# Gated DeltaNet in a two-layer encoder: the scale of the key products from a reciprocal of the sum of squares

## The chip, the cores and the metric

The kernel runs on one core of a Trainium2 chip. The metric is the device time of one execution in microseconds (us), the median of several runs. The engines are named as the profile names them: PE (TensorE matmuls), PEld (its weight loads), DVE (VectorE), ACT (ScalarE), POOL (GpSimd) and SP (SyncE, which issues the transfers).

## The reference

Two layers of an encoder work on 256 frames of width 1024 in float32. Each layer is a SwiGLU half-step, a mixing step (differential attention, a Mamba-2 head group and a gated DeltaNet head group side by side, between one input and one output projection), and a second SwiGLU half-step, with a layer norm behind each. Only the DeltaNet part is touched:

```python
def l2_normalize(x):
    return x * lax.rsqrt(jnp.sum(x * x, -1, keepdims=True) + 1e-6)

q = l2_normalize(q.reshape(bsz, s_len, G_HEADS, G_DK)) * (G_DK ** -0.5)
k = l2_normalize(k.reshape(bsz, s_len, G_HEADS, G_DK))
...
kb = kc * bc[..., None]                 # bc is beta, per frame and head
lmat = jnp.where(strict, jnp.einsum('bhcld,bhcsd->bhcls', kb, kc) * decay, 0.0)
imat = jnp.eye(CHUNK, dtype=jnp.float32) + lmat
u = lax.linalg.triangular_solve(imat, vb, left_side=True, lower=True, unit_diagonal=True)
...
v_new = u_i - jnp.einsum('bhld,bhdv->bhlv', w_i, st)
```

There are 4 heads of width 64 and chunks of 64 frames. The normalisation of k enters the products k k^T twice, so what scales them is beta / (sum of squares + 1e-6).

## The kernel before

Everything is float32. A large projection splits each weight tile into a high and a low part (`wh` by ACT in L250, `wl` by DVE in L251) and multiplies both by the high part of the activations, and `wh` also by their low part. PE is fed by such products almost all the time: L327 and L342 to L345 for the input projections, L238 to L245 for the output projections. The mixing work of a layer (attention, Mamba, DeltaNet) is written as Python generators ("chains") that are stepped between the weight units of the input projection. A `yield` with a number puts the rest of a chain that much later on a modelled clock; `until(key)` holds it until another chain has left a tile under that key. What comes out is one instruction list per engine, and each engine runs its list in order, waiting on semaphores.

The chain in question is `delta`. In both layers it does this:

- `ssps` (PE, by the helper `mm` whose line is L389): sums of squares of k and q per frame and head, as products with a selector of two columns. `ss` (DVE, L658) is that plus 1e-6, 128x16: 8 columns for k and 8 for q.
- `r8` (POOL, L660) is `ss` to the power -1/2 for all 16 columns.
- `products(b)` makes `laps`, the products k k^T and k q^T of the block `b` of 128 frames, in two PSUM tiles from the four-buffer pool `aux`, one for each half of the 128 partitions. In the program `products(1)` stands behind the four `LA` of block 0; its second tile takes the buffer that the first two of these have read.
- `d` (DVE, L682, L683) is `r8` squared times beta, for k; `nk` (L684) is `r8` times `ss`; `rq` (L685) is `r8` of q over 8, and `rq2` (L705) its square over 64.
- `LA` (DVE, L693) is `laps` times `d` times the decay tile `E`, four instructions for each block.
- `inverse` solves the triangular systems in five rounds: `TT` (L829, L835, L861), its transpose `T` (L844), `gps` and `ups` (PE), `G` (L850).
- Then the new values (`rhs` from `gv` and `nk` in L715, `vnps` on PE), the state, the outputs (`ops`, `go` in L784), and the closing norm: squares (ACT, L786), their sum (L788), `gss` (L789), a power on POOL (L430), `go` times the gate (L792), the power times `rq` (L793), `go` scaled (L794), and transposes on PE (`mTps`, L260).

Of the kernel before, what the change touches and what calls it, by code (L numbers as in the profile page):

```python
# [13 lines left out]
ALU = mybir.AluOpType  # L14
# [77 lines left out]
class Kernel:  # L92
# [553 lines left out]
    def delta(self, l, qk, sq):  # L646
        nc = self.nc
        ve = nc.vector
# [7 lines left out]
                self.mm(pss[:, at : at + 2], lhsT=sq[:, i, blk(b)], rhs=self.sel)  # L656
        ss = self.s(0, 16, "ss")
        ve.tensor_scalar(ss, pss[:, 0:16], 1e-6, None, op0=ALU.add)  # L658
        r8 = self.s(0, 16, "r8")
        nc.gpsimd.tensor_tensor(r8, ss, self.neghalf, op=ALU.pow)  # L660

        def products(b):
            pl = [self.aux(b, "laps") for _ in range(2)]
            for j in range(2):
                for p in range(2):
                    o = slice(64 * p, 64 * p + 64)
                    self.mm(
                        pl[p][:, 256 * j : 256 * j + 256],
                        lhsT=qk[o, 2 * j, blk(b)],
                        rhs=qk[o, 2 * j : 2 * j + 2, blk(b)],  # L670
                    )
            return pl

        pl = products(0)
        yield 5
        yield from self.until(("E", 0))
        ecs, erev, E = self.mx["ecs"], self.mx["erev"], self.mx["E", 0]
        pick = lambda t, a: t.rearrange("p (c a i) -> p c a i", c=4, a=2)[:, :, a, :]
        pair = lambda t: t.rearrange("p (c i) -> p c i", c=4)

        d, nk, rq = self.s(0, 8, "d"), self.s(0, 8, "nk"), self.s(0, 8, "rq")
        ve.tensor_tensor(pair(d), pick(r8, 0), pick(r8, 0), op=ALU.mult)  # L682
        ve.tensor_mul(d, d, beta)  # L683
        ve.tensor_tensor(pair(nk), pick(r8, 0), pick(ss, 0), op=ALU.mult)  # L684
        ve.tensor_scalar(pair(rq), pick(r8, 1), 0.125, None, op0=ALU.mult)  # L685
        LA = []
        for b in range(2):
            pl = products(b) if b else pl
            t = self.big([2, 2, 2, P], "LA")
            for p in range(2):  # L690
                for j in range(2):
                    hd = 2 * j + p
                    ve.scalar_tensor_tensor(  # L693
                        t[:, p, j],
                        in0=pl[p][:, 256 * j : 256 * j + 256].rearrange("p (a t) -> p a t", a=2),
                        scalar=d[:, 4 * b + hd : 4 * b + hd + 1],
                        in1=E[:, b, hd : hd + 1, :].to_broadcast([P, 2, P]),
                        op0=ALU.mult,
                        op1=ALU.mult,
                    )  # L700
            LA.append(t)
            yield 0.5

        rq2 = self.s(0, 8, "rq2")
        ve.scalar_tensor_tensor(rq2, in0=rq, scalar=1.0 / 64, in1=rq, op0=ALU.mult, op1=ALU.mult)  # L705
        de = self.s(0, 4, "de")
        ve.tensor_mul(de, d[:, 0:4], erev[:, 0, 0:4])
        self.spawn(self.k_tokens(qk, de))
        TT = yield from self.inverse(LA)
        yield from self.until("x4")  # L710
# [10 lines left out]
        for b in range(2):  # L721
            if b == 1:
# [8 lines left out]
                for p in range(2):  # L731
                    for j in range(2):
# [6 lines left out]
                            op0=ALU.mult,  # L739
                            op1=ALU.add,  # L740
                        )
                for p in range(2):
# [4 lines left out]
                        op=ALU.mult,  # L747
# [529 lines left out]
```

## Time and profile before

| what | value |
|---|---|
| time, median of 3 runs | 1086.86 us (1081.48, 1086.86, 1087.26) |
| the profiled execution's own time | 1085.23 us |
| its span, first to last instruction | 1083.5 us |
| PE busy | 1056.8 us (98%) |
| DVE busy | 754.7 us (70%) |
| ACT busy | 605.2 us (56%) |
| POOL busy | 32.0 us (3%) |
| granted TensorE clock, mean of the span | 0.991 |

The time is 1.7 us longer than the span. PE is busy nearly throughout, so what can move the time is a place at which PE stands still, or a place at which it runs at a lower clock; the other engines matter where PE waits for them. Layer 1 mixes at about 200 to 345 us, layer 2 at about 733 to 875 us.

### The profile page before, as it was taken

To read this page: it belongs to the slowest core of one execution; us is meant where nothing else is said; L and a number is where in the kernel's file an instruction comes from. 1 tells how busy PE (TensorE), PEld (TensorE's weight loads), DVE (VectorE), ACT (ScalarE), POOL (GpSimd) and SP (SyncE) were. 2 spreads that over 40 slices of the span, in tenths; PEclk is the share of its full clock that TensorE was granted. 3 is DMA by queue.
4 is the path that set the end of the run, shared out by engine and by line. 5 is a ranking of instruction groups with operands and counts; after the bars stand their busy time and mean duration, and the time that the engine had idled before them with its cause. 6 is when DMAs were issued, how large, how long until landed. Compare 5 with 4: busy or idle time off the path is not lost.

```text
span 1083.5 us, 17613 instructions
## 1 busy us (share of the span) xinstructions
PE 1056.8 (98%) x6354; PEld 898.4 (83%) x6354; DVE 754.7 (70%) x1550; ACT 605.2 (56%) x1292; POOL 32.0 (3%) x29
## 2 busy tenths in 40 slices
PE   8999999999999999999999999999989999999996
PEld 7888888787987788888878888887878878888885
DVE  5777754886776877774587777457967787777644
ACT  6687643487434566664356666446863445666540
POOL 0000000001001000000000000000010010000000
PEclk9999999998999999999999999999999999999999
DMA  9967664653234676666477666646512449666641
GB/s 274 294 180 208 191 192 143 176 157 97 60 105 145 199 216 190 195 189 195 142 222 211 190 194 191 191 105 194 177 47 72 145 132 264 181 183 187 194 136 39
DMA packets 221551, 184.34 MB, mean 170 GB/s; under 512 B 14608, under 2 KB 201368, under 8 KB 221464
## 3 DMA queue, kind: packets, MB, share of 16 engines
q1 hardware_dynamic: 221464, 183.22, 57.7%
q8 instruction: 50, 0.82, 0.3%
q14 instruction: 37, 0.30, 0.1%
HBM read 182.13 MB, written 1.05 MB: 169 GB/s over the span
## 4 chain that ended last, share of the span: by engine, by line
PE 85%; DVE 8%; issue 2%; DMA 2%; ACT 2%; POOL 1%; SPq 0%; DVEq 0%; POOLq 0%; ACTq 0%
PE ps L327 43%; PE po L238 7%; PE po L239 7%; PE po L245 7%; PE ps L345 4%; PE ps L343 4%; PE ps L342 4%; DVE wl L251 3%; DMA raw<-in_ffn_w_gu_dram 1%; PE ups L389 1%; PE gps L389 1%; POOL rsq L430 1%; PE xps L260 1%; PE yps L389 1%; PE vnps L389 1%
## 5 line engine op out<-in xcount | busy, mean ns | idle before, releaser
L251 DVE TENSOR_TENSOR wl<-raw,wh 128x512 fp32r<-128x512 f32 (+1 forms) x672 | 436.3, 681 | 195.2 <-ACT wh L250 188.4
L250 ACT CAST wh<-raw 128x512 fp32r<-128x512 f32 (+1 forms) x672 | 386.4, 616 | 206.7 <-PE po L245 100.8
L327 PE MATMUL ps<-xT,wh 128*128 128x512 f32 (+1 forms) x1600 | 492.2, 367 | 0.0
L327 PE MATMUL ps<-xT,wl 128*128 128x256 f32 x1376 | 390.5, 284 | 0.0
L327 PEld LDWEIGHTS ps<-xT,wh 128*128 128x128 f32 x1600 | 288.9, 190 | 52.9 <-issue 2.8
L327 PEld LDWEIGHTS ps<-xT,wl 128*128 128x128 f32 x1376 | 261.8, 190 | 4.0 <-issue 3.7
L238 PE MATMUL po<-wh,hT 128*128 128x512 f32 x352 | 137.7, 391 | 0.0
L239 PE MATMUL po<-wl,hT 128*128 128x512 f32 x352 | 137.0, 389 | 0.0
L245 PE MATMUL po<-wh,hT 128*128 128x512 f32 x336 | 103.6, 389 | 0.0
L342 PE MATMUL ps<-wh,xT 128*128 128x512 f32 (+2 forms) x256 | 95.2, 377 | 2.3 <-ACT wh L250 2.2
L343 PE MATMUL ps<-wl,xT 128*128 128x512 f32 (+2 forms) x256 | 94.0, 374 | 0.0
L238 PEld LDWEIGHTS po<-wh,hT 128*128 128x128 f32 x352 | 66.1, 188 | 14.5 <-DVE hh L498 1.0
L239 PEld LDWEIGHTS po<-wl,hT 128*128 128x128 f32 x352 | 66.1, 188 | 13.4
L345 PE MATMUL ps<-wh,xT 128*128 128x512 f32 (+2 forms) x256 | 73.2, 371 | 1.2 <-DVE xT L251 1.2
L245 PEld LDWEIGHTS po<-wh,hT 128*128 128x128 f32 x336 | 63.1, 188 | 13.3
L250 ACT CAST hT<-hh 128x256 fp32r<-128x256 f32 x72 | 29.3, 407 | 70.3 <-DVE hh L500 70.3
L342 PEld LDWEIGHTS ps<-wh,xT 128*128 128x128 f32 x256 | 48.6, 190 | 11.2 <-ACT wh L250 2.6
L343 PEld LDWEIGHTS ps<-wl,xT 128*128 128x128 f32 x256 | 48.4, 189 | 8.3 <-DVE wl L251 0.7
L430 POOL TENSOR_TENSOR rsq<-rs,neghalf 128x1 f32<-128x1 f32 (+2 forms) x20 | 23.8, 1192 | 995.2 <-DVE rs L428 995.2
L345 PEld LDWEIGHTS ps<-wh,xT 128*128 128x128 f32 x256 | 45.0, 188 | 9.5 <-DVE xT L251 2.1
L499 ACT ACTIVATE ga<-ga 128x256 f32<-128x256 f32 x72 | 30.1, 419 | 35.8 <-DVE ga L496 35.8
L251 DVE TENSOR_TENSOR hT<-hh,hT 128x256 fp32r<-128x256 f32 x72 | 30.5, 424 | 26.0 <-ACT hT L250 26.0
(233 smaller groups left out, 925.6 us busy)
## 6 DMA issues: line engine op xcount, KB each, us to landing
raw<-in_ffn_w_gu_dram SPq DMA_DIRECT2D x350, 256.0 KB
raw<-in_ffn_w_down_dram SPq DMA_DIRECT2D x88, 512.0 KB
raw<-in_w_in_dram SPq DMA_DIRECT2D x40, 512.0 KB
raw<-in_w_out_dram SPq DMA_DIRECT2D x16, 512.0 KB
raw<-in_w_in_dram SPq DMA_DIRECT2D x24, 256.0 KB
g<-in_ln_g_dram SPq DMA_DIRECT2D x6, 512.0 KB
b<-in_ln_b_dram SPq DMA_DIRECT2D x6, 512.0 KB
x<-in_x_dram SPq DMA_DIRECT2D x4, 256.0 KB
```

The costliest lines, as they stand in the source:

```text
L238: mm(p, lhsT=xh, rhs=wh, start=start, stop=False)
L239: mm(p, lhsT=xh, rhs=wl, start=False, stop=False)
L245: mm(p, lhsT=xl, rhs=wh, start=False, stop=False)
L250: self.nc.scalar.copy(hi, src)
L251: self.nc.vector.tensor_tensor(lo, src, hi.bitcast(F32), op=ALU.subtract)
L327: self.nc.tensor.matmul(to, lhsT=a, rhs=r, start=first and n == 0, stop=end and n == len(mms) - 1, skip_group_check=True,)
L342: mm(ps, lhsT=x(kk)[:, 0], rhs=wh[:, s], start=u["part"] == 0 and kk == 0, stop=False)
L343: mm(ps, lhsT=x(kk)[:, 0], rhs=wl[:, s], start=False, stop=False)
L345: mm(ps, lhsT=x(kk)[:, 1], rhs=wh[:, s], start=False, stop=last and kk == ks - 1)
L389: self.nc.tensor.matmul(out, lhsT=lhsT, rhs=rhs, start=start, stop=stop)
L430: nc.gpsimd.tensor_tensor(r, t, self.neghalf[:, :n], op=ALU.pow)
L499: nc.scalar.activation(a, a, AF.Silu)
```

## The change

`d` is now the reciprocal of `ss` times beta, and no longer needs `r8`. The power on POOL is issued behind it, and `nk`, `rq` and `rq2` stand behind the `LA`; `de`, which needs only `d`, stands ahead of them. One `yield 5` becomes `yield 4`.

```diff
         ve.tensor_scalar(ss, pss[:, 0:16], 1e-6, None, op0=ALU.add)
-        r8 = self.s(0, 16, "r8")
-        nc.gpsimd.tensor_tensor(r8, ss, self.neghalf, op=ALU.pow)
...
         pl = products(0)
-        yield 5
+        pick = lambda t, a: t.rearrange("p (c a i) -> p c a i", c=4, a=2)[:, :, a, :]
+        pair = lambda t: t.rearrange("p (c i) -> p c i", c=4)
+
+        d, nk, rq = self.s(0, 8, "d"), self.s(0, 8, "nk"), self.s(0, 8, "rq")
+        ve.reciprocal(pair(d), pick(ss, 0))
+        ve.tensor_mul(d, d, beta)
+        r8 = self.s(0, 16, "r8")
+        nc.gpsimd.tensor_tensor(r8, ss, self.neghalf, op=ALU.pow)
+        yield 4
         yield from self.until(("E", 0))
         ecs, erev, E = self.mx["ecs"], self.mx["erev"], self.mx["E", 0]
...
-        ve.tensor_tensor(pair(d), pick(r8, 0), pick(r8, 0), op=ALU.mult)
-        ve.tensor_mul(d, d, beta)
-        ve.tensor_tensor(pair(nk), pick(r8, 0), pick(ss, 0), op=ALU.mult)
-        ve.tensor_scalar(pair(rq), pick(r8, 1), 0.125, None, op0=ALU.mult)
         LA = []
...
+        de = self.s(0, 4, "de")
+        ve.tensor_mul(de, d[:, 0:4], erev[:, 0, 0:4])
+        ve.tensor_tensor(pair(nk), pick(r8, 0), pick(ss, 0), op=ALU.mult)
+        ve.tensor_scalar(pair(rq), pick(r8, 1), 0.125, None, op0=ALU.mult)
 
         rq2 = self.s(0, 8, "rq2")
         ve.scalar_tensor_tensor(rq2, in0=rq, scalar=1.0 / 64, in1=rq, op0=ALU.mult, op1=ALU.mult)
-        de = self.s(0, 4, "de")
-        ve.tensor_mul(de, d[:, 0:4], erev[:, 0, 0:4])
         self.spawn(self.k_tokens(qk, de))
```

The lists of the engines move with it, in the same way in both layers; the rows below are those of layer 1. First DVE, from the sums of squares to the second `LA`. Before:

```order
L658 TENSOR_SCALAR ss_2778<-ssps_2769 128x16
L682 TENSOR_TENSOR d_2856<-r_492_2780 128x8
L684 TENSOR_TENSOR nk_2857<-r_492_2780,ss_2778 128x8
L685 TENSOR_SCALAR rq_2858<-r_492_2780 128x8
L683 TENSOR_TENSOR d_2856<-d_2856,beta_2380 128x8
L705 SCALAR_TENSOR_TENSOR rq_516_2922<-rq_2858 128x8
L693 SCALAR_TENSOR_TENSOR LA_2863<-laps_2782,d_2856,ex_2565 128x256
L532 TENSOR_TENSOR xsT_2800<-xsT_2800,mxtap_2801 128x2x255
L693 SCALAR_TENSOR_TENSOR LA_2863<-laps_2782,d_2856,ex_2565 128x256
```

Now, in the changed kernel:

```order
L658 TENSOR_SCALAR ss_2778<-ssps_2769 128x16
L677 RECIPROCAL d_2786<-ss_2778 128x8
L678 TENSOR_TENSOR d_2786<-d_2786,beta_2380 128x8
L691 SCALAR_TENSOR_TENSOR LA_2861<-laps_2780,d_2786,ex_2565 128x256
L532 TENSOR_TENSOR xsT_2805<-xsT_2805,mxtap_2806 128x2x255
L691 SCALAR_TENSOR_TENSOR LA_2861<-laps_2780,d_2786,ex_2565 128x256
```

Nothing that POOL makes (`r_492`) stands ahead of `LA` any more; `nk`, `rq` and `rq2` come after the eighth `LA`, with the `de` and `TT` instructions.

Second, DVE at the end of the DeltaNet chain in the output projection; `mT` are the split parts of the merged heads, `gss` and `rs` the sums of the closing norm, `rsq` the power that POOL makes, `wl` weight splits. Before:

```order
L254 SCALAR_TENSOR_TENSOR mT_3708<-mTps_3703,nw,mT_3708 128x2x128
L251 TENSOR_TENSOR wl_3774<-raw_3516,wh_3773 128x512
L254 SCALAR_TENSOR_TENSOR mT_3661<-mTps_3656,nw,mT_3661 128x2x128
L788 TENSOR_REDUCE gss_3696<-sq_630_3694 128x8
L254 SCALAR_TENSOR_TENSOR mT_3708<-mTps_3703,nw,mT_3708 128x2x128
L789 TENSOR_TENSOR gss_3696<-gss_3696,rq_516_2922 128x8
L792 TENSOR_TENSOR go_3462<-go_3462,gw_3648 128x512
L428 TENSOR_SCALAR rs_3699<-gss_3696 128x8
L251 TENSOR_TENSOR wl_3801<-raw_3567,wh_3800 128x512
L793 TENSOR_TENSOR rsq_3701<-rsq_3701,rq_2858 128x8
L251 TENSOR_TENSOR wl_3801<-raw_3567,wh_3800 128x512
L794 TENSOR_TENSOR go_3462<-go_3462,rsq_3701 128x512
```

Now:

```order
L254 SCALAR_TENSOR_TENSOR mT_3708<-mTps_3703,nw,mT_3708 128x2x128
L788 TENSOR_REDUCE gss_3696<-sq_630_3694 128x8
L254 SCALAR_TENSOR_TENSOR mT_3661<-mTps_3656,nw,mT_3661 128x2x128
L789 TENSOR_TENSOR gss_3696<-gss_3696,rq_517_2924 128x8
L254 SCALAR_TENSOR_TENSOR mT_3708<-mTps_3703,nw,mT_3708 128x2x128
L428 TENSOR_SCALAR rs_3699<-gss_3696 128x8
L792 TENSOR_TENSOR go_3462<-go_3462,gw_3648 128x512
L793 TENSOR_TENSOR rsq_3701<-rsq_3701,rq_2788 128x8
L251 TENSOR_TENSOR wl_3774<-raw_3516,wh_3773 128x512
L794 TENSOR_TENSOR go_3462<-go_3462,rsq_3701 128x512
```

One weight split stands no longer ahead of the sum L788, the gating L792 has gone behind L428, and two weight splits have moved towards or behind L794.

Third, PE at the transposes of `go` in the same stretch; `po` are the sums of the output projection. Before:

```order
L238 MATMUL po_3731<-wh_3510,mT_2520 128x512
L239 MATMUL po_3731<-wl_3511,mT_2520 128x512
L245 MATMUL po_3730<-wh_3510,mT_2520 128x512
L245 MATMUL po_3731<-wh_3510,mT_2520 128x512
L238 MATMUL po_3713<-wh_3679,mT_3708 128x512
L260 MATMUL mTps_3753<-cst,go_3462 128x128 x4
```

Now:

```order
L238 MATMUL po_3731<-wh_3510,mT_2520 128x512
L260 MATMUL mTps_3753<-cst,go_3462 128x128 x4
L239 MATMUL po_3731<-wl_3511,mT_2520 128x512
L245 MATMUL po_3730<-wh_3510,mT_2520 128x512
L245 MATMUL po_3731<-wh_3510,mT_2520 128x512
L238 MATMUL po_3713<-wh_3679,mT_3708 128x512
```

The transposes stand four products earlier. In between, in the five rounds of `inverse` and the steps behind them, some `gps`, `ups`, `vtok` and `vnps` have moved by one to five large products, most of them later; on the queue of SP nothing has moved.

## Rows read from the trace of the kernel before

**Rows 1.** The page: the span, and the busy time of each engine.

```profile
span 1083.5 us, 17613 instructions
PE 1056.8 (98%) x6354; PEld 898.4 (83%) x6354; DVE 754.7 (70%) x1550; ACT 605.2 (56%) x1292; POOL 32.0 (3%) x29
```

**Rows 2.** The waits of PE over the whole span: who waited for whom, total in us, times, longest.

```profile
PE laps L389 <- DVE LA L693: 3.7, 2, 2.4
PE mTps L260 <- DVE go L794: 2.9, 2, 1.5
...
PE ps L342 <- ACT wh L250: 2.2, 1, 2.2
```

**Rows 3.** DVE in order of time in layer 1: start, duration, and in brackets the idle time before it and what released it.

```profile
261.19 0.17 DVE L658 TENSOR_SCALAR ss<-ssps 128x16 f32<-128x16 f32 x1 [3.72 <-PE ssps L389]
264.44 0.17 DVE L682 TENSOR_TENSOR d<-r 128x8 f32<-128x8 f32 x1 [3.08 <-POOL r L660]
...
264.68 0.16 DVE L683 TENSOR_TENSOR d<-d,beta 128x8 f32<-128x8 f32 x1
...
264.89 0.48 DVE L693 SCALAR_TENSOR_TENSOR LA<-laps,d,ex 128x256 f32<-128x256 f32 x1
265.28 0.68 DVE L532 TENSOR_TENSOR xsT<-xsT,mxtap 128x510 f32<-128x510 f32 x1
265.88 0.48 DVE L693 SCALAR_TENSOR_TENSOR LA<-laps,d,ex 128x256 f32<-128x256 f32 x1
```

**Rows 4.** POOL in order of time, the power in layer 1.

```profile
261.51 2.90 POOL L660 TENSOR_TENSOR r<-ss,neghalf 128x16 f32<-128x16 f32 x1 [8.54 <-DVE ss L658]
```

**Rows 5.** PE in order of time in layer 1: the two halves of `products(1)`, the last product between them, and the first `gps`.

```profile
261.54 1.13 PE L389 MATMUL laps<-qk 64*128 64x256 f32 x4
...
264.46 0.63 PE L327 MATMUL ps<-xT,wh 128*128 128x256 f32 x2
...
266.41 2.07 PE L389 MATMUL laps<-qk 64*128 64x256 f32 x4 [1.32 <-DVE LA L693]
...
280.14 1.12 PE L389 MATMUL gps<-T,LA 64*64 64x32 f32 x32
```

**Rows 6.** The same places of PE in layer 2.

```profile
794.89 1.13 PE L389 MATMUL laps<-qk 64*128 64x256 f32 x4
...
796.99 0.40 PE L327 MATMUL ps<-xT,wh 128*128 128x256 f32 x2
...
799.75 1.13 PE L389 MATMUL laps<-qk 64*128 64x256 f32 x4 [2.36 <-DVE LA L693]
...
810.60 1.12 PE L389 MATMUL gps<-T,LA 64*64 64x32 f32 x32
```

**Rows 7.** Stretches: length, then busy us (instructions) of PE, PEld, DVE, ACT and POOL, then the granted TensorE clock (1.00 is the upper level), DMA share, GB/s.

```profile
255.00:262.00 7.00, 7.00 (x40) 4.94 (x39) 2.64 (x6) 6.55 (x10) 0.49 (x1) 1.00 0.50 152
262.60:272.90 10.30, 8.98 (x36) 7.84 (x36) 8.41 (x25) 5.57 (x10) 1.81 (x1) 0.50 0.00 0
272.90:280.00 7.10, 7.10 (x61) 7.10 (x60) 4.59 (x10) 3.72 (x8) 0.00 (x0) 1.00 0.26 72
795.00:808.00 13.00, 10.64 (x78) 9.65 (x79) 9.99 (x30) 7.78 (x14) 2.75 (x1) 1.00 0.00 0
```

**Rows 8.** The reciprocal of line L571 (beta), the same shape as the new one: durations min/median/max in ns.

```profile
L571 DVE RECIPROCAL beta<-be x2: 203/203/203, 223.4 to 756.7; 128x8 f32<-128x8 f32 x2
```

**Rows 9.** In order of time in layer 2, DVE: the first transpose `T` of `inverse`.

```profile
809.14 0.70 DVE L844 STREAM_TRANSPOSE T<-TT 128x512 f32<-128x512 f32 x1
```

**Rows 10.** In order of time: the power of a layer norm on POOL, and the DVE instructions with two inputs in SBUF (`x` and `g`) that run beside it.

```profile
353.06 1.00 POOL L430 TENSOR_TENSOR rsq<-rs,neghalf 128x1 f32<-128x1 f32 x1 [11.70 <-DVE rs L428]
...
352.90 1.41 DVE L416 SCALAR_TENSOR_TENSOR x<-x,mv,g 128x512 f32<-128x512 f32 x2
354.22 1.41 DVE L417 SCALAR_TENSOR_TENSOR x<-x,rsq,b 128x512 f32<-128x512 f32 x2
```

**Rows 11.** In order of time, the closing norm of the DeltaNet chain in layer 1: ACT, DVE, POOL, then PE.

```profile
335.92 0.62 ACT L786 ACTIVATE sq<-go 128x512 f32<-128x512 f32 x1
...
337.45 0.68 DVE L788 TENSOR_REDUCE gss<-sq 128x8 f32<-128x512 f32 x1
338.04 0.48 DVE L254 SCALAR_TENSOR_TENSOR mT<-mTps,nw,mT 128x256 fp32r<-128x256 f32 x1
...
338.50 0.69 DVE L792 TENSOR_TENSOR go<-go,gw 128x512 f32<-128x512 f32 x1
339.11 0.17 DVE L428 TENSOR_SCALAR rs<-gss 128x8 f32<-128x8 f32 x1
...
339.35 2.01 POOL L430 TENSOR_TENSOR rsq<-rs,neghalf 128x8 f32<-128x8 f32 x1 [6.29 <-DVE rs L428]
...
340.61 0.61 PE L245 MATMUL po<-wh,mT 128*128 128x512 f32 x2
341.06 0.39 PE L238 MATMUL po<-wh,mT 128*128 128x512 f32 x1
342.91 0.63 PE L260 MATMUL mTps<-cst,go 128*128 128x128 f32 x4 [1.47 <-DVE go L794]
```

**Rows 12.** In order of time in layer 2: DVE makes the right-hand sides, PE takes them.

```profile
848.42 0.69 DVE L715 TENSOR_TENSOR rhs<-gv,nk 128x512 f32<-128x512 f32 x1 [0.45 <-ACT gv L629]
...
849.41 0.68 PE L389 MATMUL vnps<-rhs,TT 64*64 64x64 f32 x8
```

More of the change, by code (lines that the diff above doesn't have):

```diff
@@ L674, in delta @@
         pl = products(0)
-        yield 5
-        yield from self.until(("E", 0))
-        ecs, erev, E = self.mx["ecs"], self.mx["erev"], self.mx["E", 0]
         pick = lambda t, a: t.rearrange("p (c a i) -> p c a i", c=4, a=2)[:, :, a, :]
@@ L681, in delta @@
         d, nk, rq = self.s(0, 8, "d"), self.s(0, 8, "nk"), self.s(0, 8, "rq")
-        ve.tensor_tensor(pair(d), pick(r8, 0), pick(r8, 0), op=ALU.mult)
+        ve.reciprocal(pair(d), pick(ss, 0))
         ve.tensor_mul(d, d, beta)
-        ve.tensor_tensor(pair(nk), pick(r8, 0), pick(ss, 0), op=ALU.mult)
-        ve.tensor_scalar(pair(rq), pick(r8, 1), 0.125, None, op0=ALU.mult)
+        r8 = self.s(0, 16, "r8")
+        nc.gpsimd.tensor_tensor(r8, ss, self.neghalf, op=ALU.pow)
+        yield 4
+        yield from self.until(("E", 0))
+        ecs, erev, E = self.mx["ecs"], self.mx["erev"], self.mx["E", 0]
         LA = []
```

## The prediction

> **What bounds the kernel now.** I read the page first: PE is busy 1056.8 of 1083.5 us [rows 1], so an engine other than PE can only matter where PE stands still for it, or where PE runs slowly. The waits of PE come second. They are few, and the longest entry of all is the one that this change is about: PE stood 3.7 us, once in each layer, before `laps`, until DVE had made `LA` [rows 2]. The next, 2.9 us before the transposes of `go`, ends the same chain. No entry of any size names a weight split after the start (the 2.2 us before L342 is the kernel's first tile), so loads and splits run ahead of PE.
>
> Third comes DVE around that wait. `ss` is made at 261.19 and takes 0.17. Then DVE does nothing for 3.08 us until POOL has `r`, and the first `LA` starts at 264.89 [rows 3]. POOL's power takes 2.90 of it [rows 4]. Each list runs in order, so the `xsT` instructions queued behind L682 wait too. The second `LA` ends at 265.88 + 0.48 = 266.36; `laps` starts at 266.41, since its PSUM tile is the one that these two have read. PE had ended its last product at 264.46 + 0.63 = 265.09 and stood 1.32 us [rows 5]. In layer 2 it was free at 797.39 and stood 2.36 us [rows 6].
>
> The two layers run the same instructions, yet the waits differ. The stretches say why: in layer 1 the granted clock was 0.50, the lower of the two levels (1.2 GHz), from 262.6 to 272.9, and 1.00 before and after [rows 7]. What PE did before the fall was two-column `ssps` and half-row `laps`; while it was low PE stood 1.32 us and ran `laps` for 2.07 us; it rose while the large products ran without a gap. In layer 2 the same instructions kept the upper level (1.00 over 795 to 808). The wait hid part of the slow stretch in layer 1: from the first `laps` to the first `gps` took 280.14 - 261.54 = 18.60 us there, and 810.60 - 794.89 = 15.71 us in layer 2 [rows 5, 6]. So the slow stretch cost 2.89 us net.
>
> **The change part by part.** *The new way to `d`.* The reciprocal takes 0.203 us at this shape [rows 8], and L683 0.16 [rows 3]. With the 0.07 us that lies between an instruction and one that needs it (264.44 + 0.17 to 264.68), `ss` ends at 261.36, the reciprocal at 261.63, the product at 261.86, and `LA` starts at 261.91: 2.98 us earlier. The number of DVE instructions is unchanged, so no busy time is won.
>
> *The wait before `laps`.* The second `LA` then ends at 266.36 - 2.98 = 263.38, and PE comes at 265.09: no wait, 1.7 us to spare. In layer 2 the release moves from 799.7 to 796.7, and PE comes at 797.39: 0.7 us to spare. Both waits go whole: 1.32 + 2.36 = 3.68 us.
>
> *The clock in layer 1.* The `ssps` and the first `laps` are unchanged, so the fall may come again; the standing still inside the low stretch does not. No row shows that case, so I bound it. If the clock stays low as long as before, layer 1 wins its 1.32. If it stays high, layer 1 takes what layer 2 takes without its wait, 15.71 - 2.36 = 13.35, and wins 18.60 - 13.35 = 5.25. I take the middle, 3.3: the low stretch should be shorter, since the clock rose before when PE ran without a gap.
>
> *`nk`, `rq`, `rq2` moved behind `LA`.* They are read late: `nk` first at L715, 848.42 in layer 2 [rows 12]. POOL ends at 264.41 as before, and DVE gets to `nk` eight `LA` and six `xsT` instructions (0.4 or more each) after 261.91, not before 267.5. So the wait for POOL is covered by 3 us of other work; without that cover it would be the old 3.08.
>
> *What DVE must deliver next.* The first `T` ends at 809.14 + 0.70 = 809.84, and PE takes it at 810.60 [rows 6, 9]: 0.76 to spare. DVE moves 3 us, less 0.3 for the three small instructions now among the `TT`; PE moves 2.36. That holds. The later rounds are paced by PE, so both sides move together. The tightest place is L715, which ends at 849.11 against 849.41 for `vnps` [rows 12]; one large product (0.23) has moved ahead of its input and one 256-column product (0.12) ahead of `vnps`, so 0.2 us is left. At worst a few tenths there.
>
> *The end of the chain.* PE comes to the transposes of `go` four products earlier. L238 starts at 341.06 and PE is through with it at 342.91 - 1.47 = 341.44; two L245 take 341.06 - 340.61 = 0.45, so the four are 0.9 us. DVE is earlier too: the squares end at 335.92 + 0.62 = 336.54, so the sum L788, without a split ahead of it, can start at 336.6 instead of 337.45; from there to L428 lay 1.66 us, of which L792 (0.61) goes and one `mT` (about 0.4) comes: 1.44. Together 1.07 us earlier [rows 11]. The wait of 1.47 becomes about 1.3: 0.3 us for both layers. Bounds: 1.07 earlier without the move of PE gives no more than that; if DVE were not earlier, the wait would grow by 0.9 a layer. The two weight splits moved behind are used much later by PE (no wait on any `wl` in the list [rows 2]).
>
> *DVE beside POOL.* Before, DVE stood while POOL worked on `r`; now its instructions run beside it. Such a pair is in the trace: L416, with two inputs in SBUF, ran twice in 1.41 us while POOL had its power from 353.06 to 354.06, and L417, twice, took 1.41 with POOL idle [rows 10]. So the power held nothing back. The Trainium skill ("SBUF — State Buffer", "Who interferes with whom") says the opposite: GpSimd and a VectorE instruction with two SBUF inputs share a read port that is locked for a whole instruction, and the second to issue blocks. By that rule `d` times beta would stand until the power is over and the sum would be near nothing; the trace disagrees at this one-column power, and none here shows it at 16 columns.
>
> **The sum.** 2.36 + 3.3 + 0.3 = 6.0 us. Against the profiled execution's own 1085.23 this gives 1079.2. That execution lies 1.6 under the median shown (1086.86), from which the same sum gives 1080.9. The other runs lie 2.0 over it and 3.75 under it; by the 2.89 above I estimate that they differ by how often and how long the clock fell. I take 1080.0, a gain of 0.6%. About 0.5% (5.4 us) is what a measurement of this kernel can tell from no change.
>
> **The rivals.** *The waits go, the clock does as it did.* For it: the fall began before the wait. Against it: in layer 1 the clock rose only after the standing still was over. Gain 3.68 to 4.0: 1081.3 by the profile, 1083 by the median.
>
> *DVE is held by POOL.* If `d` times beta stands until the power is over at 264.41, `LA` starts near 264.65 instead of 264.89. Gain 0.24 a layer, 0.5: 1084.7 to 1086.4. [rows 10] speak against it; that the new power is three times as long speaks for it.
>
> *The clock falls in layer 2 too* (the other side). The second `laps` now follow the `ssps` without the pause but also sooner, half-row products close to two-column ones. If the clock then stays low for 10.3 us in layer 2, as in layer 1, it costs up to half, 5.15, with no wait to hide it. With layer 1 as slow as before the gains are 4.0, so this ends at 1085.23 + 1.2 = 1086.4, or 1088 by the median, slower; it decides from 8 us at the lower level. Against it: 1.00 over 795 to 808 with 2.36 us of idle in it [rows 7].
>
> **How the numbers follow.** The forecast has 0.55, the unchanged clock 0.28, POOL's hold 0.08, the fall in layer 2 0.09. The lowest case is the lowest run shown, taken as one without a fall, less both full waits (4.72) and 0.3: 1076.5. The highest that I include is 1083.2 (median less 3.68) and the few tenths at L715 and L794: 1084. Range 1076.5 to 1084. Under 1081.4 lie most of the forecast and nearly half of the unchanged clock: 0.58. Over 1092.3 lies only a longer fall: 0.03. The rest is 0.39.
>
> **What would show it.** Right: no wait of DVE on POOL ahead of `LA`; `LA` within 0.6 us of the end of `ss`; no `laps` in the waits of PE; from the first `laps` to `gps` near 13.4 us where the clock stays high; a shorter low stretch where it falls; the wait before the `go` transposes at 1.2 to 1.5 us. Wrong: a gap of DVE between the reciprocal and `LA`, a new entry of PE on `rhs` or `T`, or a low stretch in both layers.

## The result, and the profile after

The changed kernel takes 1080.3 us (median of 16 runs, 1073.88 to 1082.17); the kernel before, in the runs beside it, 1086.18 us (median of 16, 1081.48 to 1088.5). The ratio is 0.9947, 95% interval 0.9934 to 0.9960: faster by 4.3 to 7.2 us. The forecast was 1080.0. Its profiled execution took 1082.11 us, with a span of 1080.3.

The waits of PE over the whole span, as in [rows 2] of before:

```profile
PE xps L260 <- DVE x L417: 3.0, 4, 0.8
PE mTps L260 <- DVE go L794: 2.6, 2, 1.3
...
PE ps L342 <- ACT wh L250: 1.3, 1, 1.3
```

The entry `laps <- LA`, 3.7 us and the longest before, is gone. Nothing new has come: no entry names `T`, `rhs` or `nk`.

DVE in order of time in layer 1, and then POOL's power there, as in [rows 3, 4]:

```profile
261.29 0.17 DVE L658 TENSOR_SCALAR ss<-ssps 128x16 f32<-128x16 f32 x1 [3.72 <-PE ssps L389]
261.50 0.20 DVE L677 RECIPROCAL d<-ss 128x8 f32<-128x8 f32 x1
261.74 0.17 DVE L678 TENSOR_TENSOR d<-d,beta 128x8 f32<-128x8 f32 x1
261.94 0.48 DVE L691 SCALAR_TENSOR_TENSOR LA<-laps,d,ex 128x256 f32<-128x256 f32 x1
262.34 0.68 DVE L532 TENSOR_TENSOR xsT<-xsT,mxtap 128x510 f32<-128x510 f32 x1
...
261.55 2.90 POOL L680 TENSOR_TENSOR r<-ss,neghalf 128x16 f32<-128x16 f32 x1 [8.48 <-DVE ss L658]
```

`LA` starts 0.48 us after the end of `ss` (before: 3.53), while POOL is still at its power until 264.45.

PE in order of time, layer 1 and then layer 2, as in [rows 5, 6]: the first half of `products(1)`, its second half (the second `laps` of this text), the first `gps`.

```profile
261.65 1.13 PE L389 MATMUL laps<-qk 64*128 64x256 f32 x4
264.82 2.07 PE L389 MATMUL laps<-qk 64*128 64x256 f32 x4
278.08 1.12 PE L389 MATMUL gps<-T,LA 64*64 64x32 f32 x32
...
796.04 1.13 PE L389 MATMUL laps<-qk 64*128 64x256 f32 x4
798.47 1.13 PE L389 MATMUL laps<-qk 64*128 64x256 f32 x4
809.43 1.12 PE L389 MATMUL gps<-T,LA 64*64 64x32 f32 x32
```

No bracket stands behind the second `laps` any more. From the first `laps` shown to the first `gps`, which I call the core of a layer from here on, layer 1 takes 278.08 - 261.65 = 16.43 us (before 18.60) and layer 2 13.39 us (before 15.71): 2.17 and 2.32 us less, 4.49 together.

Stretches of PE: length, busy time and instructions, granted clock, DMA share, GB/s.

```profile
262.00:276.00 14.00, 14.00 (x83) 0.76 0.02 2
...
796.00:810.00 14.00, 14.00 (x120) 1.00 0.02 4
```

A mean of 0.76 over 14 us, between levels of 0.50 and 1.00, means 28 x 0.24 = 6.7 us at the lower level; before it was 10.3 [rows 7]. Layer 2 kept the upper level, as before.

The closing transposes in layer 1, as in the last row of [rows 11]: the wait is 1.29 where it was 1.47.

```profile
339.73 0.63 PE L260 MATMUL mTps<-cst,go 128*128 128x128 f32 x4 [1.29 <-DVE go L794]
```

Over both layers this entry went from 2.9 to 2.6 us. So the places of the change gained 4.49 + 0.3 = 4.8 us, yet the two profiled spans differ by only 3.2. Where the other 1.6 us went in this pair of executions, and why the medians show more, is taken up with the first experiment below.

### The profile page after: what moved, and what is told of

Same layout as the page of the kernel before. It is cut to its first block, busy times and chain, and to the rows that moved or that the text cites. A ratio compares the mean times of both kernels' runs of the same rounds, so it can differ in the third digit from the quotient of the medians.

```text
span 1080.3 us, 17610 instructions
## 1 busy us (share of the span) xinstructions
PE 1058.1 (98%) x6354; PEld 898.0 (83%) x6354; DVE 755.4 (70%) x1550; ACT 606.5 (56%) x1292; POOL 32.1 (3%) x29
## 4 chain that ended last, share of the span: by engine, by line
PE 87%; DVE 7%; ACT 2%; issue 2%; DMA 1%; POOL 1%; SPq 0%; DVEq 0%; POOLq 0%; ACTq 0%
PE ps L327 44%; PE po L238 7%; PE po L239 7%; PE po L245 7%; PE ps L342 4%; PE ps L345 4%; PE ps L343 4%; DVE wl L251 3%; PE ups L389 1%; PE gps L389 1%; POOL rsq L430 1%; PE laps L389 1%; PE xps L260 1%; DMA raw<-in_ffn_w_gu_dram 1%; PE yps L389 1%
## 5 line engine op out<-in xcount | busy, mean ns | idle before, releaser
L327 PE MATMUL ps<-xT,wh 128*128 128x512 f32 (+1 forms) x1600 | 493.2, 367 | 0.0
L327 PE MATMUL ps<-xT,wl 128*128 128x256 f32 x1376 | 390.3, 284 | 0.0
L327 PEld LDWEIGHTS ps<-xT,wh 128*128 128x128 f32 x1600 | 288.3, 190 | 54.6 <-issue 2.8
L327 PEld LDWEIGHTS ps<-xT,wl 128*128 128x128 f32 x1376 | 261.3, 190 | 3.9 <-issue 3.7
```

Of the source, the lines that this page charges most:

```text
L327: self.nc.tensor.matmul(to, lhsT=a, rhs=r, start=first and n == 0, stop=end and n == len(mms) - 1, skip_group_check=True,)
```

## The experiments

My theory was that the wait of DVE's list on POOL, passed on to PE before the second `laps`, is the whole price, with a share of the low clock. The rivals: that another part of the edit brings the time; that the clock does as it pleases.

### Both kernels once more

No edit. What was expected of the changed kernel, and then of the kernel before (the run that the first text speaks of is that with a dense product in both layers, further down):

> The changed kernel as it is, once more. Theory B of the run before it (the low stretches are a property of the execution, not of the kernel): the same order on every engine and the same waits within 0.2 us, but another length or place of the stretches at 0.50, and some of the long dense stretches at the other of two paces (0.347 or 0.353 us for a pair of products); laps to gps in layer 1 anywhere from 13.4 to 16.8 us. Theory A (they belong to the kernel): 6.8 us at 0.50 from about 263 us again, laps to gps 16.4 us. Ratio to before 0.993 to 0.997 either way.

> The kernel before as it is, once more, for its profile. If the low stretches belong to the execution: the waits before the second `laps` are again 3.7 us (up to 1.1 us more where the clock is high in layer 1, since the wait there is then longer), while the stretch at 0.50 in layer 1 has another length than 10.2 us, or one stands in layer 2. If they belong to the kernel: 10.2 us at 0.50 from 262.6 us again and none in layer 2.

Changed kernel: 1078.67 us, ratio 0.9930 (0.9906 to 0.9954). Kernel before: one run, 1081.95 us. PE in the second profile of the kernel before, layer 1 and layer 2:

```profile
259.89 1.13 PE L389 MATMUL laps<-qk 64*128 64x256 f32 x4
264.77 1.49 PE L389 MATMUL laps<-qk 64*128 64x256 f32 x4 [2.37 <-DVE LA L693]
277.12 1.12 PE L389 MATMUL gps<-T,LA 64*64 64x32 f32 x32
...
791.85 1.13 PE L389 MATMUL laps<-qk 64*128 64x256 f32 x4
796.72 1.13 PE L389 MATMUL laps<-qk 64*128 64x256 f32 x4 [2.37 <-DVE LA L693]
809.06 1.12 PE L389 MATMUL gps<-T,LA 64*64 64x32 f32 x32
```

and its stretches in layer 1 and layer 2:

```profile
262.00:276.00 14.00, 11.63 (x80) 0.88 0.00 1
...
796.00:810.00 14.00, 13.28 (x116) 0.88 0.10 25
```

The same program has 28 x 0.12 = 3.4 us at the lower level in each layer, where its first profile had 10.3 us in layer 1 and none in layer 2. In layer 1 the wait is now 2.37 us, not 1.32: the products ahead of it ran at the upper level, PE came earlier and stood longer. The cores take 17.23 and 17.21 us, 34.44 together; in the first profile 18.60 + 15.71 = 34.31.

The second profile of the changed kernel, PE in layer 1 and layer 2, and its stretches in the order of time:

```profile
259.75 1.13 PE L389 MATMUL laps<-qk 64*128 64x256 f32 x4
273.15 1.12 PE L389 MATMUL gps<-T,LA 64*64 64x32 f32 x32
...
791.09 1.13 PE L389 MATMUL laps<-qk 64*128 64x256 f32 x4
807.52 1.12 PE L389 MATMUL gps<-T,LA 64*64 64x32 f32 x32
...
262.00:276.00 14.00, 14.00 (x154) 1.00 0.14 39
790.00:796.00 6.00, 6.00 (x28) 0.71 0.14 51
796.00:810.00 14.00, 14.00 (x136) 0.88 0.13 39
```

Now layer 1 keeps the upper level and layer 2 has the low stretch. The cores take 13.40 and 16.43 us, the two numbers of the first profile changed over: 29.83 together, against 29.82. So in these profiles the sum over both layers stays the same while the layer with the low clock changes from execution to execution. The sum is no fixed property of a kernel either. In the run with only the reciprocal (further down), where PE waits before the second `laps` as in the kernel before (3.5 us), the granted clock was 0.50 for 10.2 us in layer 1 and for 3.4 us in layer 2, and the cores took 18.53 + 17.14 = 35.67 us. Of the 20 runs of the changed kernel four have a mean granted clock of 0.998 or 0.999, as the profiles without a low stretch in either layer have it (further down), and the others 0.993 to 0.996; none of the 64 runs of the kernel before beside the experiments (1079.8 to 1089.7 us) is above 0.996. By the sums of these two pairs of profiles the change is worth 34.3 to 34.4 less 29.8, or 4.5 to 4.6 us, and 0.3 at the closing: 4.8 to 4.9.

What the executions differ by besides shows in the long runs of equal products of the first FFN product (L327). The groups of PE from 930 to 1000 us, in the first profile of the kernel before, and then in the second:

```profile
L327 PE MATMUL ps<-xT,wh 128*128 128x512 f32 x199 | 70.4, 399 | 0.0
```

```profile
L327 PE MATMUL ps<-xT,wh 128*128 128x512 f32 x203 | 70.4, 391 | 0.0
```

The same instructions in the same order, without a wait and at a granted clock of 1.00, went through at 199 in 70 us in one execution and at 203 in the other. There are three such runs behind the first mixing layer, each of some 85 us. In every profile each ran at one of these two paces; the difference, measured from one group of `xps` to the next, is 1.7 us a run. The first profile of the changed kernel had two of the three at the slower pace, that of the kernel before one. That is the 1.6 us that the pair of spans lacks.

### Only the reciprocal

```
-        ve.tensor_tensor(pair(d), pick(r8, 0), pick(r8, 0), op=ALU.mult)
+        ve.reciprocal(pair(d), pick(ss, 0))
```

> Only the two DVE instructions that make `d` are changed (reciprocal of the sums times beta); the power, `nk`, `rq`, `rq2` and the yields stand where they stand in the kernel before, so the DVE list still waits for POOL ahead of LA. Theory A (the wait in DVE's list is the whole price): `d` is ready 0.5 us after `ss`, but LA still starts about 3.1 us after `ss`; PE waits before the second `laps` 1.2 to 1.5 us in layer 1 and 2.2 to 2.5 us in layer 2; ratio to before 0.998 to 1.002. Rival B (a shorter chain of arithmetic for `d` brings the time, wherever the power stands): ratio 0.993 to 0.996, as in the changed kernel.

Measured: 1086.93 us, ratio 1.0015 (0.9996 to 1.0034). DVE in layer 1, and the wait of PE over the span:

```profile
260.02 0.20 DVE L682 RECIPROCAL d<-ss 128x8 f32<-128x8 f32 x1
263.07 0.17 DVE L684 TENSOR_TENSOR nk<-r,ss 128x8 f32<-128x8 f32 x1 [2.84 <-POOL r L660]
...
263.23 0.16 DVE L683 TENSOR_TENSOR d<-d,beta 128x8 f32<-128x8 f32 x1
263.43 0.48 DVE L693 SCALAR_TENSOR_TENSOR LA<-laps,d,ex 128x256 f32<-128x256 f32 x1
...
PE laps L389 <- DVE LA L693: 3.5, 2, 2.3
```

The reciprocal is done at 260.22, but DVE's list now waits 2.84 us one instruction further, at `nk`, and the product with beta and `LA` stand behind it: the order of the list, not the data, holds them. No gain.

### Only the move

```
-        yield 5
+        yield 4
...
         ve.tensor_tensor(pair(d), pick(r8, 0), pick(r8, 0), op=ALU.mult)
         ve.tensor_mul(d, d, beta)
-        ve.tensor_tensor(pair(nk), pick(r8, 0), pick(ss, 0), op=ALU.mult)
-        ve.tensor_scalar(pair(rq), pick(r8, 1), 0.125, None, op0=ALU.mult)
...
             LA.append(t)
             yield 0.5
+        de = self.s(0, 4, "de")
+        ve.tensor_mul(de, d[:, 0:4], erev[:, 0, 0:4])
+        ve.tensor_tensor(pair(nk), pick(r8, 0), pick(ss, 0), op=ALU.mult)
+        ve.tensor_scalar(pair(rq), pick(r8, 1), 0.125, None, op0=ALU.mult)

         rq2 = self.s(0, 8, "rq2")
         ve.scalar_tensor_tensor(rq2, in0=rq, scalar=1.0 / 64, in1=rq, op0=ALU.mult, op1=ALU.mult)
-        de = self.s(0, 4, "de")
-        ve.tensor_mul(de, d[:, 0:4], erev[:, 0, 0:4])
```

> The other half: `d` is still r8*r8*beta and waits for the power, but `nk`, `rq`, `rq2` and `de` stand behind LA and the yield is 4, as in the changed kernel. Theory A: LA starts only some 0.2 us earlier than before (two small DVE instructions fewer ahead of it), the PE waits before the second `laps` are 1.1 to 1.3 us and 2.1 to 2.3 us; ratio 0.997 to 1.001. Rival B (the changed order of the later PE products and the small DVE instructions bring the time, not the wait): ratio 0.993 to 0.996 with the wait on POOL still there.

Measured: 1085.79 us, ratio 1.0007 (0.9987 to 1.0028). DVE waits 3.08 us at L682, and PE:

```profile
PE laps L389 <- DVE LA L691: 4.7, 2, 2.3
```

I had expected 1.1 to 1.3 us for layer 1; with only 3.4 us of low clock there it was 2.3, as in the second profile of the kernel before. So neither half brings anything alone. What counts is that no instruction ahead of `LA` on DVE reads the power.

### The power twice

```
         nc.gpsimd.tensor_tensor(r8, ss, self.neghalf, op=ALU.pow)
+        nc.gpsimd.tensor_tensor(r8, ss, self.neghalf, op=ALU.pow)
```

> The kernel before with the power on POOL written twice, one behind the other (same inputs, same result), so that `r8` comes 2.9 us later. Theory A (no slack is left behind this wait): PE waits before the second `laps` grow by 2.9 us, to 4.2 us in layer 1 and 5.3 us in layer 2; laps to gps 21.5 us and 18.6 us; 5.8 us more in all, ratio 1.0053, if the granted clock stays as it is in the kernel before. If the longer wait also brings the clock down in layer 2, 1.7 to 3.4 us more: ratio 1.007 to 1.0085, with a stretch at 0.50 near 797 us. Rival B (a part of the wait is taken up by slack further on): ratio below 1.003.

Measured: 1092.92 us, ratio 1.0059 (1.0033 to 1.0086), or 6.4 us (3.6 to 9.3).

```profile
266.06 0.17 DVE L683 TENSOR_TENSOR d<-r 128x8 f32<-128x8 f32 x1 [6.06 <-POOL r L661]
...
PE laps L389 <- DVE LA L694: 10.4, 2, 5.2
```

Both waits are 5.2 us, 2.9 more than the 2.37 at the upper level, in layer 1 too. No slack takes any of it up. The clock fell in both layers in this profile, for some 6.8 us in each.

### Dense products to hold the clock

The thin products are the two-column `ssps` and the half-row `laps`. What is added are dense products: one ahead of the thin ones in layer 1 (in the second run without the condition, so in both layers), and then six in both layers, where `fill()` is the same product:

```
         pss = self.aux(0, "ssps")
+        if l == 0:
+            for _ in range(1):
+                nc.tensor.matmul(pss[:, 128:512], lhsT=self.ident, rhs=self.cst[:, 0:384], start=True, stop=True)
```

```
+        fill()
+        fill()
         for b in range(2):
             for i in range(4):
                 at = 8 * b + 2 * i
                 self.mm(pss[:, at : at + 2], lhsT=sq[:, i, blk(b)], rhs=self.sel)
+                if i % 2:
+                    fill()
```

> The changed kernel with one more product on PE in layer 1 only: 128 x 384 fp32 from constants into an unused part of the sums' own bank, directly ahead of the sum-of-squares products; nothing reads it. It costs some 0.64 us. Theory A (the low clock in layer 1 comes from the thin products, two columns and half the rows, that stand together there): the stretch at 0.50 between 263 and 270 us goes, laps to gps falls from 16.4 us to about 13.4 us as in layer 2, and the kernel gains 3.0 - 0.6 = 2.4 us on the changed kernel: ratio to before about 0.9925. Rival B (the clock falls there for another reason, or at a fixed moment): the low stretch stays at 6.8 us and the kernel loses 0.6 us on the changed one: ratio about 0.995 to 0.996.

> The changed kernel with the extra product of 128 x 384 fp32 ahead of the sum-of-squares products in both layers (1.28 us in all; nothing reads it). The run with it in layer 1 alone had its stretch at 0.50 in layer 2 instead of layer 1. Theory A (the thin products bring the clock down wherever they stand bare): no stretch at 0.50 in either layer, mean granted clock about 0.997 over the runs, ratio to before 0.992 to 0.993. Rival B (where the clock falls changes from one execution of the same kernel to the next, and one dense product ahead does little): a stretch at 0.50 in one of the layers all the same, mean granted clock 0.994 to 0.995 as in the changed kernel, ratio 0.9945 to 0.996.

> The changed kernel with six of the extra products (128 x 384 fp32, 0.64 us each, nothing reads them) in both layers: two ahead of the sum-of-squares products and one behind every second of these, so that the thin products no longer stand together. 3.84 us more for PE per layer. What is asked is only whether more dense work between the thin products keeps the granted clock up, which one product ahead of them did not. If it does: no stretch at 0.50 in either layer, the stretch from the last first-batch `laps` to `gps` 13.4 us in both layers, and the kernel loses 7.7 us of extra products less some 3.0 us of clock against the changed one, ratio to before 0.998 to 1.000. If the low stretch has nothing to do with these products: 6.8 us at 0.50 in one of the layers again, 16.4 us there, ratio 1.000 to 1.003.

One in layer 1: 1080.37 us, ratio 0.9945 (0.9922 to 0.9967). One in both: 1077.62 us, 0.9929 (0.9911 to 0.9946), beside 0.9930 for the changed kernel itself in the same comparison. The low stretch, first of the kernel with one product in layer 1, then of that with one in both:

```profile
785.00:796.00 11.00, 11.00 (x51) 0.77 0.32 97
```

```profile
262.00:276.00 14.00, 14.00 (x104) 0.81 0.14 39
```

It was still there, 22 x 0.23 = 5.1 and 28 x 0.19 = 5.3 us of it in these windows and the rest beside them, once in layer 2 and once in layer 1. One product ahead of the thin ones did not hold the clock; theory A fell in that form. With six, between the thin products too: 1081.69 us, ratio 0.9982 (0.9964 to 1.0001), and in layers 1 and 2

```profile
262.00:276.00 14.00, 14.00 (x134) 1.00 0.06 11
790.00:796.00 6.00, 6.00 (x30) 1.00 0.18 60
796.00:810.00 14.00, 14.00 (x160) 1.00 0.14 39
```

the upper level throughout (the core cannot be set beside the others here, since the build moved the first `laps` behind the added products); over its ten runs the granted clock was 0.996 to 0.998, against 0.993 to 0.999 over those of the changed kernel. Eight of the ten runs have 0.997 or 0.998, where four of the twenty of the changed kernel reach that. So dense products between the thin ones make the low stretch rarer; two runs at 0.996 leave room for a short one. That the thin products standing together bring the clock down is the likeliest cause; it is not shown alone, because the build regrouped the `laps` in this kernel too. The dense products cost more than they return.

### The transposes of `go` later

```
-        yield 4
+        yield 8
         t = self.both_parts(
             [go[:, 4 * b : 4 * b + 4].rearrange("p h d -> p (h d)") for b in range(2)], "mT",
```

> The changed kernel with one number more changed: the step ahead of the closing transposes of `go` is `yield 8` instead of `yield 4`, which puts those four transposes some ten `po` products further down PE's list in both layers. Theory (PE waits for the closing norm only because the transposes stand too early; ten products of 0.23 us are 2.3 us of other work, and the split of `mT` still has some 3 us until its first product): the entry mTps <- go goes (1.3 us in each layer), 2.6 us less than the changed kernel, ratio to before about 0.992. Rival (the split of `mT` becomes the next wait): a new PE wait of up to 1.3 us on `mT` in each layer, ratio about 0.9945.

Measured: 1076.36 us, ratio 0.9905 (0.9884 to 0.9925), against 0.9930 for the changed kernel in the same comparison. The entry `mTps <- go` is gone and `mT` has none in its place. This follows the rows of the closing norm: work that PE could do meanwhile stood behind its waiting transposes.

### The transposes of `do` later too, with and without the change

```
-        yield 7
+        yield 9
         if b == 0:
             self.daT = self.big([2, 2, 2, P], "mT", F32R)
```

Put on top of the kernel with `yield 8`; then both yields put into the kernel before, beside the changed kernel with both once more:

> The changed kernel with the closing transposes of `go` later (`yield 8`, as in the run with that alone) and the transposes of the attention's `do` later too (`yield 9` instead of 7). PE waits 1.2 us in all for `do` (0.6 us, twice). If that wait goes without another in its place: 1.2 us less than with `yield 8` alone, ratio to before about 0.9895. If the transposes, moved further down, meet the sum-of-squares chain and delay it: no gain on the run with `yield 8` alone, 0.990 to 0.992.

> The kernel before (power ahead of LA, `yield 5`) with the two later transposes of the run before this one (`yield 8` ahead of those of `go`, `yield 9` ahead of those of `do`), to price the wait alone where the clock does not fall. The sums of squares now stand some 2.3 us of dense products ahead of the second `laps`, and LA needs some 4.2 us from `ss` to the release of the first `laps` bank by the rows of before: a wait of about 2 us is left in each layer. If the wait is all that the change takes away here, this kernel is 4 us slower than the next one (ratio to before about 0.988) with the granted clock at 1.00 in both layers; if the wait itself brings the clock down, a stretch at 0.50 of 3.4 to 6.8 us in one layer or both and 1.7 to 6.8 us more (0.990 to 0.994).

> The changed kernel with the same two later transposes, once more, beside the kernel before with them: no wait before the second `laps`, no stretch at 0.50 in either layer, ratio to before 0.983 to 0.986. If the high clock of the first run of this kernel was chance, a stretch of 6.8 us at 0.50 in one layer and 3.4 us more: 0.986 to 0.989.

Changed kernel with both: 1067.35 us, ratio 0.9844 (0.9817 to 0.9872), and again 1069.71 us, 0.9853 (0.9831 to 0.9875). Kernel before with both: 1073.31 us, 0.9891 (0.9869 to 0.9912). The first is the fastest version of all: by the ratios 6.6 us ahead of that with `yield 8` alone, where I had expected 1.2. The step ahead of the `do` transposes moves dense `ps` products in between the thin ones, and the clock held at 1.00 in the mixing part of both layers in all three profiles (mean 0.996 to 0.999 over the 15 runs of the three).

Layer 2 had the upper level in the profiles of five kernels, so its mixing part, from the first `xps` ahead of it to the first behind it, prices each step free of the clock and of the paces. The two rows of the kernel before:

```profile
727.88 0.60 PE L260 MATMUL xps<-cst,x 128*128 128x128 f32 x4
...
885.90 0.60 PE L260 MATMUL xps<-cst,x 128*128 128x128 f32 x4
```

The starts of the same two rows in all five:

| kernel | first `xps` ahead, us | first `xps` behind, us | between, us |
|---|---|---|---|
| before | 727.88 | 885.90 | 158.02 |
| changed | 729.01 | 884.51 | 155.50 |
| changed, `yield 8` | 723.95 | 877.93 | 153.98 |
| changed, both yields | 720.23 | 871.56 | 151.33 |
| before, both yields | 722.29 | 874.90 | 152.61 |

The change is worth 2.52 us in a layer at the upper level: the wait of 2.36 and 0.18 at the closing. `yield 8` takes off another 1.52, of which 1.3 is the wait of PE. The second yield takes off 2.65; 0.6 of it is the wait on `do`. No entry of the waits holds the other 2 us. Most of them lie in `laps`, whose products each use one half of the rows. With `yield 8` alone the two halves of `products(1)` stand apart in PE's list; with both yields they stand together. Layer 2, each group with the product behind it, first with `yield 8`, then with both:

```profile
790.92 1.13 PE L389 MATMUL laps<-qk 64*128 64x256 f32 x4
791.98 0.39 PE L327 MATMUL ps<-xT,wh 128*128 128x256 f32 x1
...
793.35 1.13 PE L389 MATMUL laps<-qk 64*128 64x256 f32 x4
794.41 0.39 PE L327 MATMUL ps<-xT,wl 128*128 128x256 f32 x1
```

```profile
785.86 1.35 PE L389 MATMUL laps<-qk 64*128 64x256 f32 x8
787.15 0.39 PE L327 MATMUL ps<-xT,wl 128*128 128x256 f32 x1
```

From start to the start behind it, two groups of four take 1.06 us each and the eight together 1.29: products of the two halves run in part side by side. In `products(0)` two groups of two, 0.63 and 0.62 us, became one of four in 0.63. Together that is 1.4 us of the 2.65; some 0.6 us stay open.

On top of both yields the change is worth only 1.28 us a layer, and that pair does not price the wait. I had expected a wait of 2 us before the second `laps` in the kernel before with both; there was none, because they do not stand behind `LA` there. They start before the first `LA` does:

```profile
789.71 1.13 PE L389 MATMUL laps<-qk 64*128 64x256 f32 x4
...
789.86 3.22 DVE L693 SCALAR_TENSOR_TENSOR LA<-laps,d,ex 128x256 f32<-128x256 f32 x8
```

What came in its place is a wait of `gps` on `T`, 0.5 us over both layers; 0.8 us more a layer are the two halves of `laps`, which stand apart in this kernel and together in the changed one, and 0.2 us stay open. The medians differ by 3.6 us.

## Why the prediction was right, and where it was not

**Right, with the numbers expected.** `LA` starts 0.48 us after the end of `ss` (by the forecast's own times, 0.55). No wait on POOL stands ahead of it. Both waits before the second `laps` went whole. Where the clock stays up, the core of a layer takes 13.39 and 13.40 us (forecast 13.35). The closing wait is 1.29 (forecast about 1.3). `nk` and `rq` wait for nothing where they stand now, and neither `T` nor `rhs` holds PE.

**POOL and DVE side by side.** L678 and L532, each with two inputs in SBUF, ran in 0.17 and 0.68 us in the middle of POOL's 2.90 us power of 16 columns; L532 took the same 0.68 before, without POOL beside it [rows 3]. The rule of the Trainium skill that I had weighed ("SBUF — State Buffer", "Who interferes with whom"), by which these would have stood until POOL was done, does not hold for these instructions, now at the full width too. That rival is out.

**Mis-sized: the term of the clock in layer 1.** I gave layer 1 as a whole 3.3 us, the middle between 1.32 and 5.25. In the pair of profiles it was 2.17, so the sum of 6.0 should have been 4.8. The step that failed is the reading behind it: I took the wait of 1.32 us and the low stretch of layer 1 as two costs of that layer, and thought that removing the one would shorten the other and so win time. The stretch did get shorter, from 10.3 to 6.7 us. But it cost the same: 18.60 - 15.71 = 2.89 us before, 16.43 - 13.39 = 3.04 after. The wait had lain inside it, and while PE stands still a low clock costs nothing: from the first `laps` shown to the second, behind the wait, it is 4.87 us in layer 1 at the low clock, 4.86 in layer 2 at the high one and 4.88 in layer 1 of the second profile. The whole difference came behind that, 13.73 against 10.85 us to `gps`. Put the other way: the true price of the wait is what the layer at the upper level shows, 2.36 us, in both layers alike; 1.32 was so small only because the slowed products ahead of it had made PE late. Twice 2.36 and the closing's 0.3 make 5.0, and in these profiles a clock that costs about 3 us in one layer or the other before and after adds nothing. I had both numbers in [rows 5, 6].

**Right by luck to that extent.** The medians differ by 5.9 us, with an interval of 4.3 to 7.2, which holds 4.8 as well as my 6.0. What the 1.1 us above 4.8 are is not shown; the mean clocks of the runs leave room for some of it, since of the two kernels only the changed one has runs at 0.998 and above. The rival that the clock does as it did came nearer in kind, but its gain of 3.7 to 4.0 used the same 1.32 and was as much too small as my sum was too large. The rival of a fall in layer 2 was half right: the clock can fall there, and did in the second profile, but then instead of in layer 1, not as well.

**The spread of the runs** I put down to the clock alone. The two paces of the long product runs, 1.7 us for each of three, are as large a part. The low end of my range took the fastest run shown as one without a fall; no run supports that, since none of those 64 of the kernel before is above a mean clock of 0.996.

## What to carry to other kernels

A wait on a slow engine is passed on by the order of the waiting engine's list: it goes only when no instruction ahead of the urgent one reads the slow result, and each half of such a change can be worth nothing alone. Read the price of a wait where the clock is high; in a low stretch the engine comes late, so the wait looks shorter and the clock dearer than either is. Where the clock falls around thin products that stand together, it is worth trying to spread them among dense ones that have to run anyway; half-row products of the two halves are better kept side by side. Here two groups of transposes put later, with no work added, gained 8 to 11 us on top of the change (ratios of 0.9930 and 0.9947 for the changed kernel, 0.9853 and 0.9844 with them): the waits of PE on `go` and `do` went, the halves of `laps` came together, and the clock held.

## What the runs showed of the hardware that I had not expected

The place and the length of a low stretch are no property of the program: the same kernel had 10.3 us in layer 1 in one execution and 3.4 us in each layer in another, and the changed one 6.7 us in layer 1 or in layer 2. And the same dense products, at a granted clock of 1.00 and without a wait, ran at one of two paces, 199 or 203 in 70 us, for a whole run of some 85 us; what picks the pace is open.
